# Two matmuls for three in the 256-token feed-forwards: one weight part against both parts of x, halves of a PSUM bank added on the way out

## The chip, the cores and the metric

The kernel runs on one core of one Trainium2 chip. The metric is device time of one execution in microseconds. The engines in what follows: PE (TensorE: matmuls, from SBUF into PSUM), DVE (VectorE), ACT (ScalarE), SP (whose queue issues the loads of weights). PSUM has eight banks of 512 float32 columns on 128 partitions.

## The reference

Two transformer blocks in a row on 256 tokens of 1024 channels, in float32. The first has two layers (a gated short convolution, then neighbourhood attention), each with a feed-forward; the second has four feed-forwards around two mixers:

```python
def swiglu(x, w_in, w_out):
    gate, up = jnp.split(x @ w_in, 2, axis=-1)
    return (jax.nn.silu(gate) * up) @ w_out

for i in range(DEPTH):                                   # second block
    x = x + 0.5 * swiglu(rms_norm(x, ffn1_norm_g[i]), ffn1_w_in[i], ffn1_w_out[i])
    ...                                                  # mixer A (i = 0) or B (i = 1)
    x = x + 0.5 * swiglu(rms_norm(x, ffn2_norm_g[i]), ffn2_w_in[i], ffn2_w_out[i])
```

The hidden width is 2816, so `w_in` is 1024 x 5632 and `w_out` 2816 x 1024.

## The kernel before

**Precision by parts.** PE works on float32r operands. Every weight and every activation is split into a high part, rounded to float32r, and the exact rest, a low part. A product is three matmuls (`mm3`): high x high, high weight x low x, low weight x high x, all summed in the same columns of PSUM. The weights are the stationary operand, the activations the moving one. Activations lie as [128 channels, 8 blocks, 256 tokens], high and low parts in two tiles (`xh`, `xl`; for the hidden values `sh`, `sl`).

**Weights.** `WeightStream` loads them in units of 1024 columns (4 blocks of 128 rows x 256 output columns; 0.5 MB) into five raw buffers. `_split` rounds a unit on ACT (`whi`) and takes the rest on DVE (`wlo`), in two pieces of 512 columns. There are four buffers each for high and low parts. `take()` hands out a unit and first records the splits of the two units behind it.

**A feed-forward of 256 tokens** (`ffn` with n = 256; once in layer 1 of the first block, four times in the second). The hidden part runs over 11 groups of 256 columns; a group takes two units for the gate and two for `up`, each 2 x 4 products. Gate and up of a block of 128 columns lie in the two halves of one bank. Then DVE multiplies a bank with the row of reciprocal norms `R` (second block only), ACT takes silu, DVE the product, and ACT and DVE split the result into `sh`, `sl`. The output part runs over 4 pairs of blocks with 22 products each (six units, the last half as long). `evac` adds a block to the residual `X` on DVE, and behind the second block of a pair `gained` makes the next stage's operand parts (`xh` on ACT, `xl` on DVE) and adds squares into `acc`. So the operands of the next stage are made pair by pair, and its first product needs blocks 0 to 3, its second unit blocks 4 to 7. In the second block the next feed-forward starts at once, and `R` is made behind its first group by `rstd_rows` from `acc` (two products with a constant `mean`, then a Newton iteration on DVE).

**Order.** The code records instructions; a scheduler of the framework puts each engine's in one fixed order. An engine runs them strictly in that order, and a wait on semaphores holds up all behind it. PSUM is parted into a pool of main banks `pm` and one of auxiliary banks `pa`: five and three in feed-forwards, four and four in the mixers; a change closes both pools and opens new ones. The feed-forward of layer 0 runs on 512 tokens (x and context together), with 512-column matmuls.

Of the kernel before, what the change touches and what calls it, by code (L numbers as in the profile page):

```python
# [11 lines left out]
ALU = mybir.AluOpType  # L12
# [54 lines left out]
class WeightStream:  # L67
    """Weights in 0.5 MB units: DRAM -> float32 -> exact float32r parts hi + lo."""
# [24 lines left out]
    def _split(self):  # L93
# [4 lines left out]
        if self.specs[self.split][3]:  # L98
            self.ready.append((v(raw), None, nk, ncol))
        else:  # L100
            hi = self.split_pool.tile([P, self.UNIT], F32R, name="whi", tag="hi")
            lo = self.split_pool.tile([P, self.UNIT], F32R, name="wlo", tag="lo")
            for c0 in range(0, n, 512):
                cs = slice(c0, min(n, c0 + 512))
                self.nc.scalar.copy(hi[:, cs], raw[:, cs])  # L105
                self.nc.vector.tensor_tensor(lo[:, cs], raw[:, cs], hi[:, cs].bitcast(F32), ALU.subtract)  # L106
            self.ready.append((v(hi), v(lo), nk, ncol))
# [13 lines left out]
def cols_units(w, c0, ncol, kblocks, raw=False):  # L121
    """Units that cover the listed blocks of rows for ncol columns, 1024 // ncol blocks each."""
# [21 lines left out]
def mix_units(w, parts):  # L144
    """A product with D columns in sums over parts of the rows."""
# [19 lines left out]
class Net:  # L165
# [27 lines left out]
    def banks(self, nmain, naux):  # L193
# [3 lines left out]
        self.pa = self.psum.enter_context(pool(name="pa", bufs=naux, space=PSUM, reuse_waits="tile"))  # L197

# [19 lines left out]

    def mm3(self, ps, ah, al, bh, bl, first, last):
# [5 lines left out]
    def split(self, hi, lo, src, scale=None):  # L225
        """hi + lo = src (times a per-partition scale), both float32r."""
# [8 lines left out]
    def newton(self, y, a, tag):  # L235
        """y = a ** -0.5."""
# [12 lines left out]
    def wstat(self, pss, xh, xl, kblocks):  # L249
        """pss[c] = W[:, c].T @ x over all listed blocks of rows, weights stationary."""  # L250
# [15 lines left out]
    def xstat_steps(self, bank, tiles, xh, xl, units):  # L266
        """x[:, tile].T @ W for two units of 256 columns, two tiles of tokens in a bank; activations stationary."""
# [7 lines left out]

    def take2(self):
        return [self.ws.take(), self.ws.take()]
# [5 lines left out]
    def partial(self, kblocks, yh, yl, evac):  # L283
        """Sums over kblocks of a product with D columns; evac(j, bank) gets blocks 2j and 2j + 1."""
        j = 0
        while j < KB // 2:
# [4 lines left out]
            banks = [self.main_bank() for _ in range(ncol // T)]  # L291
# [15 lines left out]
    def squares(self, src, acc):  # L307
        """acc + src ** 2 for src of one or two blocks [P, n]."""
# [12 lines left out]
    def rstd_cols(self, accs, ntile, tag):  # L321
        """[P, ntile]: rstd of token tile * 128 + p, from squares [P, tokens] that sum up."""
# [12 lines left out]
    def rows_from_cols(self, r, ntile):  # L335
        """PSUM [P, ntile * 128] with r as a row on every partition."""
# [8 lines left out]
    def rstd_rows(self, acc):  # L345
        """SBUF [P, 2, T]: rstd as a row on every partition, twice; acc [P, 2 * T] of squares."""
        nc = self.nc
        ps = self.aux_bank()
# [4 lines left out]
        R = self.rp.tile([P, 2, T], F32, name="R", tag="R", bufs=1)  # L353
        self.newton(R[:, 0, :], m, "rr")
        nc.vector.tensor_copy(R[:, 1, :], R[:, 0, :])
        return R

    def gained(self, j, gain, xh, xl, acc):
        """Blocks 2j and 2j + 1 of X: operand parts of gain * X, squares into acc."""
        for kb in (2 * j, 2 * j + 1):  # L360
            self.split(xh[:, kb, :], xl[:, kb, :], self.X[:, kb, :], gain[:, kb : kb + 1])
        return self.squares(self.X[:, 2 * j : 2 * j + 2, :], acc)

# [13 lines left out]
    def ada_fast(self, layer, j):  # L377
        """Columns [512 j, 512 j + 512) of the modulation of x and ctx, all on TensorE; yields before its last part."""
# [26 lines left out]
    def ada_columns(self, layer, j, row):  # L405
        """Rows [2, 512] of modulation columns into mod."""
# [7 lines left out]
    def ada_direct(self, layer, j):  # L414
        """The same in float32 products of the weights as they are."""
# [16 lines left out]
    def ada_slow(self, layer, j, vecs):  # L432
        """The same on VectorE, TensorE only sums over partitions; vecs: 1 for x alone, 2 for ctx as well."""
# [43 lines left out]
    def mod_scale(self, layer, which, half):  # L477
        """norm gain * (1 + scale) for half of the blocks."""
# [9 lines left out]
    def row_stats(self, accs, keep=None):  # L488
        """rstd of T tokens as a row on every partition: PSUM [P, T], or copied into keep."""
# [7 lines left out]
    def modulate(self, layer, which, v, src, R, blocks, xh, xl):  # L497
        """Operand parts of modulate(rms(src)) for the listed blocks, in [P, KB, T] views."""
# [17 lines left out]
    def block_squares(self, src, kb, accs):  # L516
        """accs: squares [P, T] that sum up to those of blocks 0..kb."""
# [12 lines left out]
    def ffn(self, xh, xl, sh, sl, n, parts, rows, evac, between=None):  # L530
        """evac(part, j, c, ps) gets block 2j + c of the output; n tokens; rows(): rstd rows or None."""
        nc = self.nc
        R = None
        first = True
        k8 = list(range(8))
        for part, (b0, b1) in enumerate(parts):
            for g in range(b0 // 2, b1 // 2):
                if n == 512:
                    gate = [self.main_bank() for _ in range(2)]
                    up = [self.main_bank() for _ in range(2)]  # L540
                else:
                    both = [self.main_bank() for _ in range(2)]
                    gate = [b[:, :T] for b in both]
                    up = [b[:, T:] for b in both]
                if n == 512 and first:
# [10 lines left out]
                if rows is not None and R is None:  # L556
                    R = rows()
                for c in range(2):
                    blk = 2 * g + c - b0
                    sg = self.tmp()[:, :n]  # L560
                    if R is None:
# [1291 lines left out]
```

## Time and profile before

| | |
|---|---|
| median of 3 runs | 2073.29 us (2072.49 to 2076.35) |
| span of the profiled execution | 2074.1 us |
| PE, DVE, ACT busy | 2039.3, 1481.3, 1048.2 us |
| matmuls | 15070 |
| granted clock of PE, mean | 0.996 |
| feed-forward of layer 1, hidden and output | 855 to 982, 982 to 1045 us |
| first feed-forward of block 2 | 1045 to 1235 us |
| mixer A | 1235 to 1380 us |
| second and third feed-forward | 1380 to 1570, 1570 to 1760 us |
| mixer B | 1760 to 1881 us |
| last feed-forward | 1881 to 2071 us |

The profile gives the profiled execution's span, from its first to its last instruction; that execution's own time on the device is not shown apart from it, and the three times are of other executions. The span is 0.8 us above their median. Of a group of instructions the page shows line, engine, operation, output <- inputs and shapes, the count, then the busy time in us and the mean duration in ns, then the idle time of the engine before them and what ended it. In a timeline the first number is the start in us, the second the length; x2 marks two instructions in a row, merged.

### The profile page before, as it was taken

How to read it: one execution, taken by the hardware profiler on the slowest of the kernel's cores; microseconds unless marked ns; L12 is line 12 of the kernel's file. 1: busy time of each engine (PE TensorE's matmuls, PEld its weight loads, DVE VectorE, ACT ScalarE, POOL GpSimd, SP SyncE). 2: the span in 40 equal slices, each digit the busy share in tenths (PEclk: the TensorE clock that was granted, in tenths of full speed). 3: DMA queues.
4: the chain of work that ended last, by engine and by line, in shares of the span. 5: the costliest groups of instructions: out<-in, count | busy, mean ns of one | idle time of the engine just before them, and what ended most of it. 6: DMA issues, size and time to landing. Idle time of an engine off the chain costs nothing. (4 is left out here: it accounts for less than half of the span.)

```text
span 2074.1 us, 38366 instructions
## 1 busy us (share of the span) xinstructions
PE 2039.3 (98%) x15070; PEld 1912.2 (92%) x15070; DVE 1481.3 (71%) x3177; ACT 1048.2 (51%) x2136; POOL 4.1 (0%) x24
## 2 busy tenths in 40 slices
PE   7999999999999999999999999999999999999999
PEld 3888888888899999999999999999999999989999
DVE  5979998666378778755576657777657665887664
ACT  4534533323355557655455446545545545675443
POOL 0000000000000000000000000000000000000000
PEclk9999999999999999999999999999999999999999
DMA  7746566665254333455565564555556555425554
GB/s 242 231 146 194 182 204 193 222 197 190 83 182 134 91 105 127 156 184 178 181 190 184 177 182 123 158 169 190 180 178 191 185 174 183 143 82 171 185 175 132
DMA packets 327461, 351.33 MB, mean 169 GB/s; under 512 B 12592, under 2 KB 301488, under 8 KB 327280
## 3 DMA queue, kind: packets, MB, share of 16 engines
q1 hardware_dynamic: 327280, 348.88, 53.3%
q8 instruction: 118, 1.93, 0.4%
q14 instruction: 63, 0.52, 0.1%
HBM read 347.78 MB, written 1.05 MB: 168 GB/s over the span
## 5 line engine op out<-in xcount | busy, mean ns | idle before, releaser
L106 DVE TENSOR_TENSOR wlo<-wraw,whi 128x512 fp32r<-128x512 f32 x1121 | 736.5, 685 | 378.6 <-ACT whi L105 374.2
L105 ACT CAST whi<-wraw 128x512 fp32r<-128x512 f32 x1121 | 646.6, 617 | 696.1 <-issue 353.8
L221 PE MATMUL pm<-xh,whi 128*128 128x256 f32 (+1 forms) x2472 | 753.2, 306 | 3.8 <-ACT xh L229 3.2
L222 PE MATMUL pm<-xl,whi 128*128 128x256 f32 (+1 forms) x2472 | 753.4, 305 | 0.2 <-DVE xl L230 0.2
L223 PE MATMUL pm<-xh,wlo 128*128 128x256 f32 (+1 forms) x2472 | 752.9, 305 | 0.0
L221 PEld LDWEIGHTS pm<-xh,whi 128*128 128x128 f32 x2472 | 467.3, 189 | 27.3 <-ACT xh L229 4.4
L222 PEld LDWEIGHTS pm<-xl,whi 128*128 128x128 f32 x2472 | 467.4, 189 | 21.5 <-DVE xl L230 0.6
L223 PEld LDWEIGHTS pm<-xh,wlo 128*128 128x128 f32 x2472 | 467.3, 189 | 21.0
L221 PE MATMUL pm<-sh,whi 128*128 128x256 f32 (+1 forms) x1264 | 368.3, 291 | 0.0
L223 PE MATMUL pm<-sh,wlo 128*128 128x256 f32 (+1 forms) x1264 | 368.2, 291 | 0.0
L222 PE MATMUL pm<-sl,whi 128*128 128x256 f32 (+1 forms) x1264 | 367.9, 291 | 0.0
L221 PEld LDWEIGHTS pm<-sh,whi 128*128 128x128 f32 x1264 | 242.1, 192 | 4.9 <-issue 0.5
L223 PEld LDWEIGHTS pm<-sh,wlo 128*128 128x128 f32 x1264 | 242.1, 192 | 4.2 <-DVE wlo L106 0.2
L222 PEld LDWEIGHTS pm<-sl,whi 128*128 128x128 f32 x1264 | 242.1, 192 | 4.0
L446 DVE SCALAR_TENSOR_TENSOR ada_acc<-wraw,sil,ada_acc 128x512 f32<-128x512 f32 x224 | 159.1, 746 | 21.1 <-DMA wraw<-in_w_ada 19.8
L221 PE MATMUL pm<-whi,xh 128*128 128x256 f32 x576 | 164.9, 286 | 0.0
L223 PE MATMUL pm<-whi,xl 128*128 128x256 f32 x576 | 163.4, 284 | 0.0
L222 PE MATMUL pm<-wlo,xh 128*128 128x256 f32 x576 | 163.0, 283 | 0.1
L221 PEld LDWEIGHTS pm<-whi,xh 128*128 128x128 f32 x576 | 109.6, 190 | 2.6 <-issue 2.5
L222 PEld LDWEIGHTS pm<-wlo,xh 128*128 128x128 f32 x576 | 109.5, 190 | 0.3 <-DVE wlo L106 0.3
L223 PEld LDWEIGHTS pm<-whi,xl 128*128 128x128 f32 x576 | 109.5, 190 | 0.0
L229 ACT CAST sh<-t 128x256 fp32r<-128x256 f32 (+1 forms) x140 | 63.0, 450 | 79.9 <-DVE t L570 68.9
(391 smaller groups left out, 1998.3 us busy)
## 6 DMA issues: line engine op xcount, KB each, us to landing
wraw<-in_ffn_w_in SPq DMA_DIRECT2D x264, 512.0 KB, 4.4
wraw<-in_ffn_w_out SPq DMA_DIRECT2D x128, 512.0 KB, 3.5
wraw<-in_w_ada SPq DMA_DIRECT2D x96, 512.0 KB, 4.4
wraw<-in_a_w_in SPq DMA_DIRECT2D x28, 512.0 KB, 3.6
wraw<-in_conv_w_in SPq DMA_DIRECT2D x24, 512.0 KB, 4.7
wraw<-in_attn_w_qkv SPq DMA_DIRECT2D x24, 512.0 KB, 4.2
wraw<-in_conv_w_out SPq DMA_DIRECT2D x16, 512.0 KB, 4.0
wraw<-in_ffn_w_out SPq DMA_DIRECT2D x28, 256.0 KB, 2.7
```

Of the source, the lines that this page charges most:

```text
L105: self.nc.scalar.copy(hi[:, cs], raw[:, cs])
L106: self.nc.vector.tensor_tensor(lo[:, cs], raw[:, cs], hi[:, cs].bitcast(F32), ALU.subtract)
L221: mm(ps, ah, bh, start=first, stop=False)
L222: mm(ps, ah, bl, start=False, stop=False)
L223: mm(ps, al, bh, start=False, stop=last)
L229: nc.scalar.copy(hi, src)
L446: nc.vector.scalar_tensor_tensor(accs[v], w[:, kk, :], c, accs[v], ALU.mult, ALU.add)
```

## The change

High and low parts of an operand lie side by side: one tile `x2` [128, 8, 2, 256], and `s2` likewise. `pair_unit` multiplies a high weight block with both parts in one 512-column matmul, which fills a bank (half 0: high x high, half 1: high x low), and adds low weight x high part into half 0 with a 256-column matmul. ACT copies the halves 1 of a group's four banks out (`low`), DVE adds them to the halves 0 (`h`) and multiplies by `R`, then silu, product and split go over two blocks at a time. In the output both halves are added to `X`, one after the other. PSUM is two halves of four banks (`half_banks`), used in turn by groups. `rstd_rows` runs after two units of the first group instead of four. `_split` takes a whole unit of 1024 columns in one instruction on ACT and one on DVE, in all stages. The mixers' last output part (`mixer_out`) and `memory_values` use auxiliary banks, and the pools are not opened anew before `mixer_out`.

```diff
 class WeightStream:  # _split
-            for c0 in range(0, n, 512):
-                cs = slice(c0, min(n, c0 + 512))
-                self.nc.scalar.copy(hi[:, cs], raw[:, cs])
-                self.nc.vector.tensor_tensor(lo[:, cs], raw[:, cs], hi[:, cs].bitcast(F32), ALU.subtract)
+            self.nc.scalar.copy(hi[:, :n], raw[:, :n])
+            self.nc.vector.tensor_tensor(lo[:, :n], raw[:, :n], hi[:, :n].bitcast(F32), ALU.subtract)
...
+    def half_banks(self, first):
+        self.psum.close()
+        self.pg = [self.psum.enter_context(self.tc.tile_pool(name=f"pg{i}", bufs=1, space=PSUM, reuse_waits="tile")) for i in range(2)]
+        self.turn = first
+    def group_banks(self):
+        i = self.turn
+        self.turn = 1 - i
+        return self.pg[i].tile([P, 4, 2, T], F32, name=f"pg{i}", tag=f"pg{i}")
...
+    def pair_unit(self, unit, pss, x2, done, nblocks):
+        hi, lo, nk, ncol = unit
+        for c in range(ncol // P):
+            cs = slice(c * P, (c + 1) * P)
+            for kk in range(nk):
+                kb = done + kk
+                self.nc.tensor.matmul(pss[c], hi[:, kk, cs], x2[:, kb], start=kb == 0, stop=False)
+                self.nc.tensor.matmul(pss[c][:, 0, :], lo[:, kk, cs], x2[:, kb, 0, :], start=False, stop=kb == nblocks - 1)
...
+    def ffn_pairs(self, hp, x2, rows, evac, first):
...
+        def hidden(g, ps):
+            low = wide("low", 1)
+            nc.scalar.copy(low, ps[:, :, 1, :])
+            h = wide("h", 2)
+            nc.vector.tensor_tensor(h, ps[:, :, 0, :], low, ALU.add)
+            if rows is not None:
+                nc.vector.tensor_tensor(h, h, env["R"][:, None, :].to_broadcast([P, 4, T]), ALU.mult)
+            yield
+            sg = two(self.tmp())
+            nc.scalar.activation(sg, h[:, 0:2, :], AF.Silu)
+            s = two(self.tmp())
+            nc.vector.tensor_tensor(s, h[:, 2:4, :], sg, ALU.mult)
+            yield
+            self.split(s2[:, 2 * g : 2 * g + 2, 0, :], s2[:, 2 * g : 2 * g + 2, 1, :], s)
+            yield
...
+        for g in range(HB // 2):
+            after = None
+            for u in range(4):
+                unit = self.ws.take()
+                self.pair_unit(unit, [ps[:, u // 2 * 2 + c] for c in range(2)], x2, u % 2 * 4, KB)
+                next(behind, None)
+                if g == 0 and u == 1:
+                    after = self.group_banks()
+                    if rows is not None:
+                        env["R"] = rows(after[:, 0].rearrange("p a t -> p (a t)"))
+            behind = hidden(g, ps)
+            next(behind)
+            ps = after if after is not None else self.group_banks()
...
 def ffn2  # evac
-            nc.vector.scalar_tensor_tensor(x, ps, 0.5, x, ALU.mult, ALU.add)
+            for i in range(2):
+                nc.vector.scalar_tensor_tensor(x, ps[:, i, :], 0.5, x, ALU.mult, ALU.add)
...
 def mixer_out
-    for _ in net.partial(ks, yh, yl, add):
+    for _ in net.partial(ks, yh, yl, add, net.aux_bank):
...
-        net.banks(5, 3)
         return mixer_out(net, MIX_A[-1], yh, yl, gain)
```

How the order moves at the entry from the second to the third feed-forward of block 2 (1570 us before), engine by engine. PE first, in the first group of the third feed-forward; `acc` and `mean` make the statistics. Before:

```order
L221 MATMUL pm<-xh,whi 128x256
L222 MATMUL pm<-xl,whi 128x256
L223 MATMUL pm<-xh,wlo 128x256
L349 MATMUL pa<-acc,mean 128x256
L350 MATMUL pa<-acc,mean 128x256
L221 MATMUL pm<-xh,whi 128x256
L222 MATMUL pm<-xl,whi 128x256
```

Now (the names x_13956 and pg_... are `x2` and a half of PSUM):

```order
L295 MATMUL pg_15646<-x_13956,whi 128x512
L296 MATMUL pg_15646<-x_13956,wlo 128x256
L295 MATMUL pg_15646<-x_13956,whi 128x512
L296 MATMUL pg_15646<-x_13956,wlo 128x256
L370 MATMUL pg_15691<-acc,mean 128x256
L371 MATMUL pg_15691<-acc,mean 128x256
L295 MATMUL pg_15646<-x_13956,whi 128x512
L296 MATMUL pg_15646<-x_13956,wlo 128x256
```

Two matmuls stand for three, and the statistics stand after two units of the group instead of four.

ACT at the same place: `whi` rows are splits of weights, `xh` (now x_13956) the operand of the third feed-forward, the row behind it the squares. Before:

```order
L232 ACTIVATE xh<-X,pk 128x256 x2
L313 ACTIVATE t<-X 128x512
L105 CAST whi<-wraw 128x512 x11
L232 ACTIVATE xh<-X,pk 128x256 x2
L313 ACTIVATE t<-X 128x512
```

Now:

```order
L242 ACTIVATE x_13956<-X,pk 128x256 x2
L335 ACTIVATE t<-X 128x512
L103 CAST whi<-wraw 128x1024
L103 CAST whi<-wraw 128x512
L103 CAST whi<-wraw 128x1024 x5
L242 ACTIVATE x_13956<-X,pk 128x256 x2
L335 ACTIVATE t<-X 128x512
```

Eleven half units were the last two units of the output part (one of them short) and four of the next stage; now five of the next stage stand ahead of the casts of blocks 6 and 7.

DVE at the same place; `X` rows are the additions to the residual, L352 (now L373) reads the statistics. Before:

```order
L106 TENSOR_TENSOR wlo<-wraw,whi 128x512 x9
L1137 SCALAR_TENSOR_TENSOR X<-pm,X 128x256 x2
L106 TENSOR_TENSOR wlo<-wraw,whi 128x512
L233 SCALAR_TENSOR_TENSOR xl<-X,pk,xh 128x256 x2
L106 TENSOR_TENSOR wlo<-wraw,whi 128x512
L318 TENSOR_TENSOR acc<-acc,t 128x512
L106 TENSOR_TENSOR wlo<-wraw,whi 128x512 x8
L352 TENSOR_SCALAR t<-pa 128x256
```

Now:

```order
L104 TENSOR_TENSOR wlo<-wraw,whi 128x1024 x3
L1193 SCALAR_TENSOR_TENSOR X<-pg_15359,X 128x256
L104 TENSOR_TENSOR wlo<-wraw,whi 128x1024
L1193 SCALAR_TENSOR_TENSOR X<-pg_15359,X 128x256 x3
L104 TENSOR_TENSOR wlo<-wraw,whi 128x1024
L243 SCALAR_TENSOR_TENSOR x_13956<-X,pk,x_13956 128x256 x2
L340 TENSOR_TENSOR acc<-acc,t 128x512
L373 TENSOR_SCALAR t<-pg_15691 128x256
```

The fourth unit of the next stage stands between the four additions, and the fifth ahead of the two low parts.

More of the change, by code (lines that the diff above doesn't have):

```diff
@@ L290, in partial @@
                 units.append(self.ws.take())
-            banks = [self.main_bank() for _ in range(ncol // T)]
+            banks = [(bank or self.main_bank)() for _ in range(ncol // T)]
             for c in range(ncol // P):
@@ L527, in block_squares, with ffn @@
         return [new]
-    def ffn(self, xh, xl, sh, sl, n, parts, rows, evac, between=None):
+    def ffn(self, xh, xl, sh, sl, parts, evac, between):
         nc = self.nc
-        R = None
         first = True
@@ L537, in ffn @@
             for g in range(b0 // 2, b1 // 2):
[L538 to L545, printed above, removed]
+                gate = [self.main_bank() for _ in range(2)]
+                up = [self.main_bank() for _ in range(2)]
+                if first:
                     units = [self.ws.take() for _ in range(4)]
@@ L1254, in mixer_out @@
 def mixer_out(net, ks, yh, yl, gain):
-    nxh, nxl = net.next_x()
+    nx2 = net.next_x()
     st = {"acc": None}
```

132 lines of the change are left out of this document (68 added, 64 removed).

## The prediction

> **What bounds the kernel now.** First the page's span and engine shares, then the waits of TensorE (PE), then a table by stretch, then the order in time at the places where one stage hands over to the next.
>
> ```profile
> span 2074.1 us, 38366 instructions
> PE 2039.3 (98%) x15070; PEld 1912.2 (92%) x15070; DVE 1481.3 (71%) x3177; ACT 1048.2 (51%) x2136; POOL 4.1 (0%) x24
> PEclk9999999999999999999999999999999999999999
> PE pm L221 <- ACT xh L229: 3.2, 3, 1.9
> PE pm L221 <- DVE X L1246: 0.9, 1, 0.9
> ```
>
> PE is busy for 98% of the span at a granted clock that never falls below nine tenths, and the largest waits of its product line L221 are single microseconds. So the time is the sum of what each matmul takes, and a busy share does not say what that is: matmuls overlap. The distance from one start to the next does. In a table by stretch, x counts the matmuls that touch the stretch, so the distance is (length + duration of one) / count; the durations stand in the groups by line.
>
> ```profile
> L221 PE MATMUL pm<-xh,whi 128*128 128x256 f32 x1952 | 551.2, 283 | 3.0 <-ACT xh L229 2.3 <-ACT whi L105 0.6
> L221 PE MATMUL pm<-xh,whi 128*128 128x512 f32 x512 | 199.2, 392 | 0.8 <-ACT xh L229 0.8
> core 0: us, PE busy (x), PEclk, DMA share, GB/s
> 451.00:471.00 20.00, 20.00 (x90) 1.00 0.64 203
> 862.00:980.00 118.00, 118.00 (x986) 1.00 0.61 192
> 985.00:1043.00 58.00, 58.00 (x486) 1.00 0.59 186
> 1395.00:1505.00 110.00, 110.00 (x929) 1.00 0.58 181
> 1510.00:1569.00 59.00, 59.00 (x494) 1.00 0.58 183
> ```
>
> The first stretch is the 512-token feed-forward: (20 + 0.39) / 90 = 226.6 ns for 512 columns. The others are feed-forwards of 256 tokens: 118.28 / 986 = 120.0 and 58.28 / 486 = 119.9 ns in the one of attention (hidden, output), 110.28 / 929 = 118.7 and 59.28 / 494 = 120.0 ns in one of block 2. Doubling the columns adds 106.6 ns, so about 13.4 ns of each matmul does not depend on its columns.
>
> **The change, part by part.** *A. Three matmuls become two.* A feed-forward has 11 x 4 x 8 = 352 products in the hidden part and 8 x 22 = 176 in the output, 2640 in all five. Each was three 256-column matmuls and becomes one of 512 and one of 256: 226.6 + 120.0 = 346.6 ns. Before: 3 x 120.0 = 360.0, and 3 x 118.7 = 356.1 in the hidden parts of block 2. Attention's feed-forward gains 528 x 13.4 = 7.1 us; each of the four others 352 x 9.5 + 176 x 13.4 = 5.7 us. Sum 29.9 us, all of it on the path, since PE has no slack there. No row has the two widths in turn. Bounds: with 118.7 for the narrow one the sum is 29.9 + 2640 x 0.0013 = 33.3 us; if columns alone counted (the same 768 are streamed) it is 0. I take the first, since both widths have a steady pace of their own.
>
> The Trainium skill speaks against this term: "TensorE: Matmul & The Clock Gate", section "Back-to-back issue gap", gives N / 2.4 + 2.5 ns at full clock, by which a matmul saved is worth 2.5 ns and all 2640 some 6.6 us. The rows above, 120.0 and 226.6 against its 109.2 and 215.8, do not agree with it here; its constant is the isolated gap without a weight load, and the measurement decides.
>
> *B. The vector and scalar work of a group.* It is hidden if a group of four units still fits in PE's 32 x 0.3466 = 11.1 us.
>
> ```profile
> L106 DVE TENSOR_TENSOR wlo<-wraw,whi 128x512 fp32r<-128x512 f32 x132 | 86.8, 686 | 58.5 <-ACT whi L105 57.7
> L570 DVE TENSOR_TENSOR t<-t 128x256 f32<-128x256 f32 x22 | 9.3, 421 | 4.9 <-ACT t L567 4.9
> L105 ACT CAST whi<-wraw 128x512 fp32r<-128x512 f32 x132 | 75.7, 617 | 72.3 <-issue 40.5 <-PE pm L222 29.6 <-ACT whi L105 1.4
> L229 ACT CAST sh<-t 128x256 fp32r<-128x256 f32 x22 | 8.9, 404 | 6.9 <-DVE t L570 6.9
> 1573.30 1.89 DVE L106 TENSOR_TENSOR wlo<-wraw,whi 128x512 fp32r<-128x512 f32 x3
> 1578.77 1.14 ACT L105 CAST whi<-wraw 128x512 fp32r<-128x512 f32 x2 [1.66 <-PE pm L222]
> ```
>
> VectorE (DVE) takes 686 ns for 512 columns and 421 for 256; back to back it issues one every (1.89 - 0.69) / 2 = 0.60 us. So I estimate a 1024-column instruction at 686 + 2 x 265 = 1216 ns, one every 1.13; its bounds are the same 1.13 and two halves, 1.20. ScalarE (ACT) by the same working: 617 + 2 x 213 = 1043 ns, one every 0.95 (two halves: 1.14 - 0.62 + 0.52 = 1.04). A group costs DVE four splits, the addition of the halves and the product with `R` at 1.13 and two of 512 at 0.60, 8.0 us; ACT four splits and `low` at 0.95 and two of 512, 5.8 us. Both fit into 11.1, and PSUM's other half is needed only a group later. In the output a block pair costs DVE 5 x 1.13 + 0.60 for weights, four additions, two low parts and the squares, under 10 us of PE's 44 x 0.3466 = 15.3. I cost B at nothing inside the stages; if that cover fails, PE waits group by group (rival 4).
>
> *C. The hand-over from one feed-forward to the next.* Here PE has always had the next operand in time:
>
> ```profile
> 1570.02 0.28 PE L223 MATMUL pm<-sh,wlo 128*128 128x256 f32 x1
> 1570.14 0.28 PE L221 MATMUL pm<-xh,whi 128*128 128x256 f32 x1
> 1570.22 0.62 ACT L105 CAST whi<-wraw 128x512 fp32r<-128x512 f32 x1 [0.30 <-PE pm L222]
> 1570.75 0.90 ACT L232 ACTIVATE xh<-X,pk 128x256 fp32r<-128x256 f32 x2
> 1570.04 0.75 DVE L1137 SCALAR_TENSOR_TENSOR X<-pm,X 128x256 f32<-128x256 f32 x2
> 1571.31 0.88 DVE L233 SCALAR_TENSOR_TENSOR xl<-X,pk,xh 128x256 fp32r<-128x256 f32 x2
> 1572.70 0.68 DVE L318 TENSOR_TENSOR acc<-acc,t 128x512 f32<-128x512 f32 x1
> 1581.53 0.59 PE L349 MATMUL pa<-acc,mean 128*128 128x256 f32 x2
> ```
>
> The low parts of blocks 6 and 7 end at 1572.19. PE reaches block 6 after its first unit and blocks 4 and 5 of the second, 30 matmuls or 3.5 us after 1570.14, at 1573.7: 1.5 us of slack. In the new order (shown with the change) ACT splits one more unit, the fifth of the next stage, ahead of the two operand casts. That unit's buffer is the first unit's, free when PE has done its last wide matmul: 7 x 0.347 + 0.39 = 2.8 us after the start. Counting from PE's start in the stage from 1570: the cast of weights ends at 2.86 + 1.04 = 3.9; DVE's split of that unit, which also stands ahead, takes 3.95 to 5.1; the low part of block 6 ends at 5.1 + 0.48 = 5.6. PE needs it at 10 x 0.347 = 3.5: a wait of 2.1 us. At the entry from attention's feed-forward the DVE split stands behind the low parts, so only ACT's place counts: operand cast 3.8 to 4.3, low part 4.8, wait 1.4 us. At the entry to mixer A the fourth unit's split stands between the four additions: cast 0.3 to 1.35, split to 2.6, three additions (0.335 apart) to 3.6, low parts at 4.1 and 4.8 against 3.7 and 4.5, 0.8 us. At the entry to mixer B no split stands between, and the mixers hand over to feed-forwards with one addition as before: nothing. Sum 4.3 us; bounds 0 (if the scheduler's spacing holds ACT's work earlier than I think) and, with every one of the seven entries paying 2.1, 14.7.
>
> The statistics rows (L349) move from after four units to after two. `acc` would come 1.3 us behind block 7's low part, at about 6.6, and PE, itself held to 5.6, reaches them at 7.6: nothing. They are the same matmuls as before and stay.
>
> *D. Gaps that the old PSUM pools made.*
>
> ```profile
> 1234.41 0.28 PE L223 MATMUL pm<-sh,wlo 128*128 128x256 f32 x1
> 1235.32 0.36 PE L221 MATMUL pm<-xh,whi 128*128 128x256 f32 x1 [0.64 <-ACT whi L105]
> 1367.88 0.28 PE L223 MATMUL pm<-yh,wlo 128*128 128x256 f32 x1
> 1369.04 0.35 PE L221 MATMUL pm<-yh,whi 128*128 128x256 f32 x1 [0.88 <-DVE X L1246]
> ```
>
> Before mixer A and before its last output part PE stood for 0.91 and 1.16 us between starts, beyond the 0.12 of a matmul 0.8 and 1.0. At both places banks changed hands; afterwards the mixer starts in the half that has long been empty, and the output part uses banks that are open already. I take 0.7 and 0.9 back (ends 0 and 1.8), 1.6 us.
>
> *E. The ends.* In the last feed-forward the final block takes two additions instead of one:
>
> ```profile
> 2070.58 0.28 PE L223 MATMUL pm<-sh,wlo 128*128 128x256 f32 x1
> 2070.89 0.42 DVE L1137 SCALAR_TENSOR_TENSOR X<-pm,X 128x256 f32<-128x256 f32 x1 [0.29 <-PE pm L223]
> ```
>
> so 0.4 us more. At the start, where the first units are awaited, a unit is whole after 1.04 + 1.22 = 2.26 us on ACT and DVE, against 0.62 + 0.52 + 0.69 = 1.83 in two halves: 0.4 us more once (ends 0 and 1). In the mixers the split of a whole unit frees 0.07 us of DVE and 0.1 of ACT, and can hold up a short chain by 0.53 more; I take these as equal.
>
> **Sum.** 2074.1 - 29.9 + 4.3 - 1.6 + 0.8 = 2047.7 us for this execution. Its span lies 0.8 above the median of the three times, 2073.29, so 2047 us.
>
> **Rivals.**
> 1. *No new waits, narrow matmuls at 118.7.* Terms C and E vanish and A is 33.3: 2074.1 - 33.3 - 1.6 = 2039. The unchanged slack of 1.5 us speaks for it, the order of ACT against it.
> 2. *Entries and mixers cost more.* Attention's mixing and both mixers take some 107 units. If one in five of their splits holds the chain up by its extra 0.53 us, that is 11 us; the entries at twice the price add 4: 2047.7 + 15 = 2063, less still than before. For it: DVE is busy there for four fifths of the time and PE waits on short chains. Against it: DVE and ACT have less to do in all.
> 3. *Columns alone count.* The pair takes as long as the triple, A is 0 and the waits stay: 2074.1 + 4.3 - 1.6 + 0.8 = 2077.6, within 0.2% of before. It needs the 13.4 ns to belong to the 256 columns, against the 512-column row. The Trainium skill's gap, quoted above ("TensorE: Matmul & The Clock Gate", "Back-to-back issue gap"), comes near this case: by it the time would be 2071.
> 4. *The other side: DVE becomes the bound in the hidden groups.* If a 1024-column instruction took p instead of 1.13, a group would cost DVE 6 p + 1.2. Above p = 1.65 that is over PE's 11.1, and above p = 1.73 (55 groups, each losing 0.48) the whole gain of 26.4 is gone. At p = 2.0 it is 13.2, 2.1 lost in each of 55 groups: 2047.7 + 116 = 2163. Its place would be the addition that reads four banks of PSUM and the product with a repeated `R`. Against it: the row of 128x512 `t<-pm,R`, which reads PSUM, is no slower than the split of weights:
>
> ```profile
> L566 DVE TENSOR_TENSOR t<-pm,R 128x512 f32<-128x512 f32 x22 | 15.0, 683 | 0.0
> ```
>
> **Chances.** The forecast 0.70, rival 1 0.10, rival 2 0.12, rival 3 0.03, rival 4 0.05. Rivals 3 and 4 together are under one in ten, so the range reaches over most of 1 and half of 2: 2038 to 2059. About 0.2%, 4 us, is what a measurement of this kernel can tell from no change. Faster 0.70 + 0.10 + 0.12 = 0.92, the same 0.03, slower 0.05.
>
> **What would show it.** A: matmuls start 346 to 347 ns apart per pair in the hidden and output stretches; 360 would be rival 3. B: PE has no wait on `low`, `h` or weights inside a stage; waits that return every 11 to 12 us would be rival 4, and the mean of the 1024-column DVE groups tells its price at once (1216 ns, or near 2000). C: waits of PE on the low part of the operand, once at each of three entries, 1 to 2 us. D: the two gaps at mixer A are gone. The prediction fails if the pair is not the sum of its two widths, or if the mixers' stretches change by more than some microseconds.

## The result: 3.1% slower, and the profile after

The changed kernel takes 2139.38 us (median of four runs, 2133.12 to 2142.92) against 2072.89 for the kernel before in the same runs: a ratio of 1.0311, interval 1.0291 to 1.0331. The forecast was 2047 us, faster.

Three lines of the page after, to be held against the first ones of the prediction:

```profile
span 2137.1 us, 31972 instructions
PE 2051.0 (96%) x12430; PEld 1799.1 (84%) x12430; DVE 1517.3 (71%) x2568; ACT 1043.2 (49%) x1535; POOL 4.1 (0%) x24
PEclk9999999999999999999999999999999999999999
```

PE has 2640 matmuls fewer and is busy 12 us longer, in a span 63 us longer. The clock in tenths of the span still reads 9 everywhere: a loss of some microseconds at a time doesn't show there. (Nor did it in the kernel before: its clock was 0.50 from 1250.3 to 1253.7 us, so the prediction's "never falls below nine tenths" holds for the fortieths of the span only.) The waits of PE show the loss (what PE waits for, then total, times, longest, in us):

```profile
PE pg L295 <- DVE X L1193: 28.6, 8, 3.6
PE pa L349 <- DVE acc L340: 11.4, 1, 11.4
PE pg L295 <- DVE X L534: 7.7, 2, 3.8
PE pa L349 <- DVE acc L546: 5.5, 2, 4.0
PE pa L364 <- DVE t L362: 3.7, 3, 2.7
PE pg L295 <- DVE x L243: 3.2, 2, 2.0
```

The last line is the wait that the prediction named (term C). The second is no news: the kernel before has it too, with 11.7 us. The first and the third were not in the prediction: ten stops of 3.55 to 3.84 us, two in each of the five feed-forwards, where a wide matmul waits for DVE's additions to `X`. One of them in the order of time, PE first, then DVE:

```profile
1208.46 0.28 PE L296 MATMUL pg<-s,wlo 128*128 128x256 f32 x1
1212.34 0.76 PE L295 MATMUL pg<-s,whi 128*128 128x512 f32 x1 [3.60 <-DVE X L1193]
```

```profile
1208.38 1.23 DVE L104 TENSOR_TENSOR wlo<-wraw,whi 128x1024 fp32r<-128x1024 f32 x1 [1.60 <-ACT whi L103]
1209.52 0.42 DVE L1193 SCALAR_TENSOR_TENSOR X<-pg,X 128x256 f32<-128x256 f32 x1
1209.85 1.22 DVE L104 TENSOR_TENSOR wlo<-wraw,whi 128x1024 fp32r<-128x1024 f32 x1
1210.98 1.21 DVE L1193 SCALAR_TENSOR_TENSOR X<-pg,X 128x256 f32<-128x256 f32 x3
```

The matmul at 1212.34 is the first of the output's second pair of blocks. It writes banks 2 and 3 of a half; the additions read banks 0 and 1. It starts only when the fourth addition is done, because the four banks are one tile (`pg`). The additions take 1.6 us, the two weight splits among them 2.4. By stretch, in the same place (busy time and count of PE, of its weight loads, of DVE, ACT and POOL, then the granted clock):

```profile
1205.00:1208.40 3.40, 3.40 (x21) 2.99 (x20) 1.25 (x2) 1.56 (x2) 0.00 (x0) 1.00 0.33 99
1208.40:1212.20 3.80, 0.34 (x2) 0.02 (x1) 3.77 (x7) 1.55 (x2) 0.00 (x0) 0.90 0.71 231
1212.20:1215.00 2.80, 2.66 (x8) 2.31 (x9) 1.30 (x3) 1.03 (x2) 0.00 (x0) 0.50 0.75 215
1215.00:1218.00 3.00, 3.00 (x11) 2.53 (x10) 0.00 (x0) 0.34 (x1) 0.00 (x0) 0.50 0.02 6
1218.00:1221.00 3.00, 3.00 (x18) 2.62 (x17) 1.23 (x1) 0.86 (x2) 0.00 (x0) 0.95 0.00 0
```

Behind this stop the clock is 0.50 for some 6 us, and 3 us hold 11 matmuls instead of 18. So this stop costs more than its wait. The Trainium skill has this on its page "TensorE: Matmul & The Clock Gate", section "HAM oscillation — how this bites in real kernels": idle gaps of more than about 3.4 us send the array back to half clock. These rows agree with it. The trace as a whole agrees only in part: behind two of the ten stops the clock stayed at 1.00, and behind one wait of 1.98 us it fell (rows in the last section).

The stages from one first matmul to the next, in us, of the kernel before, the changed one and two of the experiments below:

| stage | before | after | three mends | with banks in turn |
|---|---|---|---|---|
| up to attention's feed-forward | 853.5 | 869.1 | 853.3 | 853.9 |
| attention's feed-forward | 191.5 | 197.8 | 190.1 | 185.3 |
| first of block 2 | 190.3 | 201.1 | 188.1 | 184.5 |
| mixer A | 145.3 | 147.2 | 144.3 | 142.9 |
| second, third of block 2 | 189.5, 189.5 | 195.5, 201.5 | 186.6, 188.2 | 184.8, 185.2 |
| mixer B | 121.5 | 124.3 | 124.2 | 123.4 |
| last feed-forward | 189.4 | 195.7 | 186.5 | 184.7 |
| behind the last matmul's start | 3.5 | 4.9 | 4.8 | 4.9 |

### The profile page after: what moved, and what is told of

The parts are those of the page before. It is cut to its first block, busy times and chain, and to the rows that moved or that the text cites. A ratio compares the mean times of both kernels' runs of the same rounds, so it can differ in the third digit from the quotient of the medians.

```text
span 2137.1 us, 31972 instructions
## 1 busy us (share of the span) xinstructions
PE 2051.0 (96%) x12430; PEld 1799.1 (84%) x12430; DVE 1517.3 (71%) x2568; ACT 1043.2 (49%) x1535; POOL 4.1 (0%) x24
## 4 chain that ended last, share of the span: by engine, by line
PE 84%; DVE 8%; ACT 4%; issue 2%; DMA 2%; SPq 0%; DVEq 0%; ACTq 0%
PE pg L295 29%; PE pg L296 15%; PE pm L232 11%; PE pm L231 11%; PE pm L233 11%; DVE wlo L104 3%; PE pa L231 2%; PE pa L232 1%; PE pa L233 1%; ACT whi L103 1%; DVE ada_acc L466 1%; DMA wraw<-in_w_ada 1%; DVE X L1193 1%; ACT t L528 1%; PE pa L443 0%
## 5 line engine op out<-in xcount | busy, mean ns | idle before, releaser
L104 DVE TENSOR_TENSOR wlo<-wraw,whi 128x1024 fp32r<-128x1024 f32 (+1 forms) x575 | 686.4, 1195 | 416.5 <-ACT whi L103 414.3
L103 ACT CAST whi<-wraw 128x1024 fp32r<-128x1024 f32 (+1 forms) x575 | 589.8, 1027 | 767.9 <-PE pg L295 279.0
L295 PE MATMUL pg<-x,whi 128*128 128x512 f32 x1408 | 496.6, 395 | 3.2 <-DVE x L243 3.2
L296 PE MATMUL pg<-x,wlo 128*128 128x256 f32 x1408 | 398.7, 283 | 0.0
L295 PE MATMUL pg<-s,whi 128*128 128x512 f32 x880 | 326.1, 412 | 36.3 <-DVE X L1193 28.6
L295 PEld LDWEIGHTS pg<-x,whi 128*128 128x128 f32 x1408 | 264.8, 188 | 65.2 <-DVE x L243 4.1
L296 PEld LDWEIGHTS pg<-x,wlo 128*128 128x128 f32 x1408 | 265.1, 188 | 0.1
L231 PE MATMUL pm<-xh,whi 128*128 128x512 f32 (+1 forms) x576 | 216.1, 380 | 1.2 <-ACT xh L239 1.2
L231 PEld LDWEIGHTS pm<-xh,whi 128*128 128x128 f32 x576 | 108.7, 190 | 23.9 <-ACT xh L239 2.3
L233 PEld LDWEIGHTS pm<-xh,wlo 128*128 128x128 f32 x576 | 108.6, 189 | 21.7 <-DVE wlo L104 1.3
L232 PEld LDWEIGHTS pm<-xl,whi 128*128 128x128 f32 x576 | 108.7, 189 | 20.7 <-DVE xl L240 0.5
L231 PE MATMUL pm<-sh,whi 128*128 128x256 f32 (+1 forms) x384 | 119.2, 311 | 0.2 <-ACT whi L103 0.2
```

What stands on the lines that cost most here:

```text
L103: self.nc.scalar.copy(hi[:, :n], raw[:, :n])
L104: self.nc.vector.tensor_tensor(lo[:, :n], raw[:, :n], hi[:, :n].bitcast(F32), ALU.subtract)
L231: mm(ps, ah, bh, start=first, stop=False)
L232: mm(ps, ah, bl, start=False, stop=False)
L233: mm(ps, al, bh, start=False, stop=last)
L295: self.nc.tensor.matmul(pss[c], hi[:, kk, cs], x2[:, kb], start=kb == 0, stop=False)
```

## The experiments

The theories: (1) the output's pairs wait for each other through a tile; (2) `memory_values` in auxiliary banks stands behind the norm statistics; (3) splits of a whole unit hold up short chains; (4) wide and narrow matmuls in turn don't keep the pace that each has by itself. Each stands against the rival that its expectation names.

**New halves in the output.** The changed kernel, with

```diff
-            if j == 2:
+            if j > 0:
                 ps = self.group_banks()
-            pss = [ps[:, j % 2 * 2 + c] for c in range(2)]
+            pss = [ps[:, c] for c in range(2)]
```

> One edit to the changed kernel: every output pair takes a new half of PSUM, so no pair shares a tile with the pair before it. Theory 1 (a half is one tile, and the second pair of a half waits for all additions that read the first, although they read other banks): the ten stops of about 3.75 us go, and with them the slow matmuls behind each. The five output parts, 364 us together, come to 5 x 176 x 0.353 = 311, so 2139 - 53 = 2086 us, between 2080 and 2092. Rival (the additions themselves are late, or DVE is full there, so the wait only moves to another instruction): less than 10 us, above 2129.

2082.8 us, 1.0042 of before (1.0029 to 1.0056): 56.6 us off the changed kernel. The first two lines of the waits above are gone. DVE does the same in the same order in the same place:

```profile
1196.86 0.42 DVE L1193 SCALAR_TENSOR_TENSOR X<-pg,X 128x256 f32<-128x256 f32 x1
1197.19 1.21 DVE L104 TENSOR_TENSOR wlo<-wraw,whi 128x1024 fp32r<-128x1024 f32 x1
1198.32 1.20 DVE L1193 SCALAR_TENSOR_TENSOR X<-pg,X 128x256 f32<-128x256 f32 x3
```

and PE goes from the last matmul of one pair of blocks to the first of the next without a stop:

```profile
1195.80 0.28 PE L296 MATMUL pg<-s,wlo 128*128 128x256 f32 x1
1195.92 0.40 PE L295 MATMUL pg<-s,whi 128*128 128x512 f32 x1
```
The additions were never late for anything but the shared tile: theory 1 is shown. The five output parts fall from 363.8 to 310.8 us, 53.0, of which the waits were 36.3. The clock behind them explains most of the rest: in these parts of the changed kernel it was 0.50 for 41 us, some 37 of them with matmuls running, and at 12 matmuls instead of 19 in 3.4 us (rows in the last section) that is 14 us, an estimate.

**Main banks for memory_values.** The changed kernel, with

```diff
 def memory_values
-        bank = net.aux_bank()
+        bank = net.main_bank()
```

> One edit to the changed kernel: memory_values takes main banks again, as before the change; by the order its first product then stands on TensorE ahead of the norm statistics instead of behind them. Theory 2 (the changed banks cost the entry to attention's feed-forward 7 us of idle and some slow matmuls behind it): attention's feed-forward starts 7 to 10 us earlier, near 861 instead of 869, and the time is 2139 - 9 = 2130 us, between 2127 and 2133. Rival (the 14 us by which that feed-forward starts late come from the attention stage ahead of it, and the products only move): within 2 us of 2139.

2139.3 us, no difference to the changed kernel: a miss. The products did move ahead of the statistics, but attention's feed-forward begins at 869.7, since a new wait stands before it:

```profile
PE pg L295 <- DVE mvl L243: 8.8, 1, 8.8
```

`mvl` is made from the banks of these products; they lie in the half of PSUM that the feed-forward opens first. The rival isn't shown by that either, so the theory was tried once more with other banks, further down.

**Whole-unit splits in the kernel before.** The kernel before, with

```diff
-            for c0 in range(0, n, 512):
-                cs = slice(c0, min(n, c0 + 512))
-                self.nc.scalar.copy(hi[:, cs], raw[:, cs])
-                self.nc.vector.tensor_tensor(lo[:, cs], raw[:, cs], hi[:, cs].bitcast(F32), ALU.subtract)
+            self.nc.scalar.copy(hi[:, :n], raw[:, :n])
+            self.nc.vector.tensor_tensor(lo[:, :n], raw[:, :n], hi[:, :n].bitcast(F32), ALU.subtract)
```

> The kernel before with one edit: a weight unit is split in one instruction of 1024 columns on ACT and one on DVE instead of two each. Theory 3 (whole-unit splits hold up short chains in attention's mixing and the two mixers): 5 us later at attention's feed-forward, 2 and 3 us in mixers A and B and about 2 at entries between feed-forwards, so 2073 + 10 = 2083 us, between 2078 and 2088. Rival (the splits cost nothing, and those 10 us come from the other parts of the change or from the order that the scheduler chose): within 4 us of 2073.

2084.7 us, 1.0047 (1.0032 to 1.0062): 10.1 us slower by this alone. Attention's feed-forward begins at 859.2 instead of 853.5, mixer A takes 1.9 more, mixer B 1.4; the feed-forwards are the same to 0.1 us. (In mixer B the clock was 0.50 for 3.4 us, which it wasn't there in the kernel before, so how much of the 1.4 is the splits' is not shown.) Theory 3 is shown, and its place is the mixing, not the hand-over between feed-forwards.

**Runs of one width.** New halves in the output, and in `pair_unit`

```diff
             for kk in range(nk):
                 kb = done + kk
                 self.nc.tensor.matmul(pss[c], hi[:, kk, cs], x2[:, kb], start=kb == 0, stop=False)
+            for kk in range(nk):
+                kb = done + kk
                 self.nc.tensor.matmul(pss[c][:, 0, :], lo[:, kk, cs], x2[:, kb, 0, :], start=False, stop=kb == nblocks - 1)
```

> The kernel with new halves in the output, and a second edit: within a unit and a column block the four 512-column matmuls stand first and the four 256-column ones behind them, instead of in turn. Theory 4 (taking the widths in turn costs some 6 ns a pair: in the changed kernel 233 + 120 = 353 where each width by itself would give 226.6 + 120.0 = 346.6): pairs at 347 to 349 ns, 2640 x 0.005 = 13 us less than the kernel with new halves alone, so 13 us below it. Rival (the rest of 6 ns belongs to the wide matmul whatever stands beside it, or to DVE and PSUM traffic): the same pace of 353 and the same time within 3 us.

2079.8 us, 1.0029 (1.0018 to 1.0040), 3.0 below the kernel with new halves, where 13 were expected. Four wide ones in a row still start 232 to 233 ns apart and four narrow ones 118 to 119: neither side is met. Either a wide matmul is slower in the new layout, or four in a row are too few.

**Splits of 512 columns again.** New halves in the output, and the diff of the whole-unit splits the other way round.

> The kernel with new halves in the output, with weights split in two instructions of 512 columns again. Theory 3 as the run on the kernel before left it (whole-unit splits cost 5.7 us ahead of attention's feed-forward, 1.9 in mixer A, 1.4 in mixer B): 2082.8 - 9 = 2074 us, between 2070 and 2077; attention's feed-forward starts near 862 instead of 867.5. It also holds that the entry waits between feed-forwards (1.4 and 2.1 us of PE on the low part of the operand) come from the whole unit that ACT casts first: they fall below 0.5 us. Rival (in the new PSUM order the short chains are held up by something else): within 4 us of 2082.8.

2070.4 us, 0.9985 (0.9976 to 0.9993): 12.4 us off, at the lower edge of what was expected. Attention's feed-forward begins at 860.1. The entries improve only in part: the waits on the low part of the operand are 0.3 and 0.6 at one of them (one stop of 1.4 before) and 1.1 at the other (2.0 before), not below 0.5. ACT still casts a unit of weights between the two operand casts there; half the size, it costs half the wait.

**Own banks for memory_values.** New halves in the output, whole-unit splits, and

```diff
-        net.banks(5, 3)
+        net.banks(4, 2)
+        net.pv = net.psum.enter_context(tc.tile_pool(name="pv", bufs=2, space=PSUM, reuse_waits="tile"))
 def memory_values
-        bank = net.aux_bank()
+        bank = net.pv.tile([P, 512], F32, name="pv", tag="pv")
```

> The kernel with new halves in the output, and two banks of the upper half kept for memory_values alone (pools of 4, 2 and 2), whole-unit splits as in the changed kernel. Theory 2 in its second form (memory_values on main banks gains 7 us and loses 8.8 again, because the first half of PSUM that the feed-forward opens then waits for DVE to read those banks; in banks of the upper half of its own it would keep the gain): the products stand ahead of the norm statistics, no wait on mvl, attention's feed-forward starts near 860 instead of 867.5 and the time is 2082.8 - 8 = 2075 us, between 2072 and 2078. Rival (the chain to the feed-forward's operand ends at the same time whatever PE does meanwhile): the products merely fill the idle time, less than 3 us.

2077.0 us, 1.0014 (1.0005 to 1.0023): 5.8 us below the kernel with new halves, and attention's feed-forward begins at 860.9 instead of 867.5. In the changed kernel PE stood idle there while DVE made the statistics, with the products of `memory_values` (L231, `pa`) queued behind, and the clock was 0.50 from 849.7 to 859.9:

```profile
845.83 0.28 PE L233 MATMUL pm<-oh,wlo 128*128 128x256 f32 x1
850.14 0.59 PE L349 MATMUL pa<-mean,acc 128*128 128x1 f32 x2 [4.04 <-DVE acc L546]
...
854.75 1.22 PE L364 MATMUL pa<-t,ones 128*128 128x256 f32 x2 [2.73 <-DVE t L362]
855.41 0.78 PE L231 MATMUL pa<-whi,xl 128*128 128x256 f32 x1
```

In the banks of their own (`pv`) they stand ahead and fill that time, as in the kernel before, and the statistics no longer wait:

```profile
846.26 0.28 PE L231 MATMUL pv<-whi,xl 128*128 128x256 f32 x1
...
850.59 0.28 PE L349 MATMUL pa<-mean,acc 128*128 128x1 f32 x2
```

Theory 2 holds in this second form.

**The three mends together** (new halves, own banks, splits of 512).

> New halves in the output, own banks for memory_values, and weights split by 512 columns: the three mends together. If all three theories hold and add up: 2139.4 - 56.6 - 9 - 8 = 2066 us, 0.4% below the kernel before, between 2062 and 2070. If the mends overlap in attention (the same idle time counted twice): 2071 to 2074, no difference to the kernel before that can be measured.

2064.1 us, 0.9950 (0.9937 to 0.9963), faster than before. The gains add up. This is the change without its three side effects, and so the measure of what it is worth itself: some 10 us, 8 to 13 by the interval of the ratio.

**Patterns.** New halves in the output, and in each feed-forward another order of matmuls, read by time per product.

```diff
 def pair_unit  # wide(c, kk): high weight times x2; slim(c, kk): low weight times the high part
+        if self.stage == 0:    # per product: wide, then low weight times both parts, 512 columns as well
+        if self.stage == 1:    # three 256-column matmuls (the first product of a block: wide, slim)
+        if self.stage == 2:    # per unit: all wide ones, then all slim ones
+        if self.stage == 3:    # wide, slim, slim, wide
+        if self.stage == 4:    # per row block: wide on both banks, slim on both banks
```

> The kernel with new halves in the output; each of the five feed-forwards issues its matmuls in another pattern, to be read as time per product. First, all 512 columns wide (low weight times both parts of x, one part more than needed); second, three 256-column matmuls in the new layout, as before the change; third, eight wide ones, then eight narrow ones per unit; fourth, wide narrow, narrow wide, so that like stands beside like; fifth, wide on one bank, wide on the other, then both narrow. Theory 4 mended (each width keeps 226.6 and 120.0 only in a row of its like, and each change of width costs 2 to 4 ns): 453, 360 or 356, 348, 350, 350 ns. Rival (a wide matmul costs 233 in the new layout whatever stands beside it): 466, 356 to 360, 351 to 353, 353, 353 ns.

One stretch of each, the first feed-forward with two (hidden, output), the others of their output parts:

```profile
880.00:1020.00 140.00, 140.00 (x619) 115.97 (x618) 71.85 (x69) 60.72 (x69) 0.00 (x0) 1.00 0.47 144
1030.00:1100.00 70.00, 70.00 (x310) 57.97 (x310) 34.48 (x45) 25.69 (x32) 0.00 (x0) 1.00 0.48 147
1240.00:1290.00 50.00, 50.00 (x421) 49.72 (x420) 29.84 (x42) 23.36 (x30) 0.00 (x0) 1.00 0.62 185
1570.00:1620.00 50.00, 50.00 (x288) 43.90 (x288) 31.46 (x44) 23.93 (x31) 0.00 (x0) 1.00 0.60 189
1760.00:1810.00 50.00, 50.00 (x289) 43.65 (x288) 30.32 (x42) 22.86 (x29) 0.00 (x0) 1.00 0.63 194
2070.00:2115.00 45.00, 45.00 (x260) 39.23 (x259) 24.46 (x30) 16.85 (x18) 0.00 (x0) 1.00 0.53 163
```

As in the prediction, (length + one matmul) / count is the distance; one is 0.39 us, 0.28 or, of a pair, 0.34 on the mean. All wide: 140.39 / 619 and 70.39 / 310, 227 ns a matmul, 454 a product: the new layout costs a wide matmul nothing, and the rival is out. Runs of a unit 349.6, mirrored 348.4, by banks 348.8, against 351 to 354 for wide and narrow in turn (rows two runs below). That is theory 4 in direction, but the cost doesn't follow the number of changes of width: runs of eight change least and are not the quickest; in the hidden part of the same feed-forward they gained nothing (90.34 / 514 x 2 = 351.5 ns, from 1460 to 1550 us). The triple here took 50.28 / 421 x 2.955 matmuls a product = 353, less than the 360 in the kernel before, so the pair seemed to gain nothing at all; hence the run after next.

**The three mends, and banks in turn.**

```diff
 def pair_unit
+        cols = [slice(c * P, (c + 1) * P) for c in range(ncol // P)]
+        for kk in range(nk):
+            kb = done + kk
+            for c, cs in enumerate(cols):
+                self.nc.tensor.matmul(pss[c], hi[:, kk, cs], x2[:, kb], start=kb == 0, stop=False)
+            for c, cs in enumerate(cols):
+                self.nc.tensor.matmul(pss[c][:, 0, :], lo[:, kk, cs], x2[:, kb, 0, :], start=False, stop=kb == nblocks - 1)
```

> The kernel with the three mends, and a fourth: in a unit the matmuls go wide on one bank, wide on the other, narrow on the one, narrow on the other. The look at the patterns gave 347.6 ns a product for this order against 353.4 for wide and narrow in turn. If that holds in all five feed-forwards: 2640 x 0.0055 = 14 us less, 2064 - 14 = 2050 us, between 2046 and 2055. Rival (the pace of single stages shifts, but waits behind the matmuls take it back): within 4 us of 2064.

2050.4 us, 0.9883 (0.9869 to 0.9896): the best of all, 1.2% below the kernel before, and 13.7 us of it by an order of instructions alone. In the hidden and output parts of two feed-forwards:

```profile
890.00:970.00 80.00, 80.00 (x462) 69.79 (x461) 55.61 (x80) 47.63 (x80) 0.00 (x0) 1.00 0.63 189
980.00:1035.00 55.00, 55.00 (x318) 47.98 (x317) 35.69 (x63) 27.37 (x49) 0.00 (x0) 1.00 0.60 187
1390.00:1480.00 90.00, 90.00 (x518) 78.81 (x517) 68.89 (x97) 53.91 (x90) 0.00 (x0) 1.00 0.62 189
1495.00:1545.00 50.00, 50.00 (x289) 43.60 (x289) 31.77 (x59) 25.42 (x47) 0.00 (x0) 1.00 0.63 196
```

348 to 349 ns a product in all four, near the 346.6 of term A.

**The three mends, but triples.** `pair_unit` in turn as in the change, past a block's first product with

```diff
-                self.nc.tensor.matmul(pss[c], hi[:, kk, cs], x2[:, kb], start=kb == 0, stop=False)
+                    for i in range(2):
+                        self.nc.tensor.matmul(pss[c][:, i, :], hi[:, kk, cs], x2[:, kb, i, :], start=False, stop=False)
```

> The kernel with the three mends, but every product past the first of a block as three 256-column matmuls again, into the same halves of a bank; the work on the way out stays. It asks what two matmuls for three are worth by themselves. If nothing (the pattern run had 353.4 ns for three narrow ones in an output part, as much as the pair): 2064 us, between 2061 and 2069. If the triple takes 360 in this layout too, as in the kernel before: 2640 x 0.0066 = 17 us more, 2081.

2074.2 us, 0.9997 (0.9988 to 1.0006), between the two: triples cost 0.47% more than pairs in turn, 9.7 us by the two ratios (each with about 3 us of interval). The stretches of the triples, and below them those of the pairs (the kernel with the three mends):

```profile
890.00:970.00 80.00, 80.00 (x645) 78.75 (x644) 53.04 (x78) 45.45 (x78) 0.00 (x0) 1.00 0.61 185
985.00:1040.00 55.00, 55.00 (x455) 54.73 (x455) 32.98 (x61) 26.18 (x48) 0.00 (x0) 1.00 0.61 188
1390.00:1480.00 90.00, 90.00 (x733) 88.57 (x732) 68.41 (x97) 53.81 (x89) 0.00 (x0) 1.00 0.62 188
1505.00:1560.00 55.00, 55.00 (x455) 54.72 (x455) 34.16 (x62) 26.34 (x49) 0.00 (x0) 1.00 0.60 187
```

```profile
890.00:970.00 80.00, 80.00 (x455) 69.38 (x454) 53.86 (x77) 46.36 (x78) 0.00 (x0) 1.00 0.62 186
985.00:1040.00 55.00, 55.00 (x313) 47.72 (x312) 34.24 (x62) 27.20 (x50) 0.00 (x0) 1.00 0.61 188
1390.00:1480.00 90.00, 90.00 (x514) 78.94 (x514) 68.93 (x97) 54.26 (x89) 0.00 (x0) 1.00 0.63 190
1505.00:1555.00 50.00, 50.00 (x285) 43.41 (x284) 32.12 (x59) 25.07 (x45) 0.00 (x0) 1.00 0.61 194
```

With 2.875 matmuls a product in the hidden parts and 2.955 in the output ones (a block's first product is a pair), the triple takes 357.8, 359.0, 354.1 and 359.0 ns; the pair 353.1, 353.6, 351.5 and 353.3. Over the parts that is 352 x 4.7 + 4 x 352 x 2.6 + 880 x 5.5 ns = 10.2 us. The 353 of the pattern run was one stage's peculiarity: the same stage has it here too (62.2 us for 176 products), no other has (63.2). Why is open.

**Banks in turn in the kernel before.** In `wstat_unit` the same loops, three kinds of products by two banks.

> The kernel before with one edit: the three matmuls of a product alternate between the two banks of a unit (high weights times high x on both banks, then the next kind on both). If the order and not the widths makes part of the pace, the 256-column triples fall from 360 and 356 towards 350 ns: 2640 x 0.007 = 18 us less, 2056. If a narrow matmul takes 118.7 to 120.0 in a row of its like, in whatever bank: 2074, within 4 us.

2084.8 us, 1.0046 (1.0032 to 1.0061). In a hidden part of attention's feed-forward and one of block 2:

```profile
890.00:980.00 90.00, 90.00 (x753) 90.00 (x752) 50.45 (x93) 45.66 (x94) 0.00 (x0) 1.00 0.60 182
1395.00:1505.00 110.00, 110.00 (x926) 109.89 (x925) 77.72 (x145) 57.84 (x115) 0.00 (x0) 1.00 0.60 187
```

90.28 / 753 = 119.9 and 110.28 / 926 = 119.1 ns: narrow matmuls keep their pace whatever bank they go to, as the second theory had it. So what banks in turn mend is the mixture of widths. The time lies some 11 us above even the second expectation. The edit also reorders the convolution and the mixers' projections, and the loss lies outside the feed-forwards: that of attention begins 6.7 us later, both mixers take longer. Why was not followed further.

## Why the prediction was wrong

The forecast lies 92.4 us below the measured time. Four steps account for most of it.

1. *Term B, "PSUM's other half is needed only a group later ... I cost B at nothing inside the stages": 56.6 us.* In the hidden groups the sentence held: DVE's and ACT's prices came out as estimated (1223 and 1050 ns against 1216 and 1043), and nothing waited ahead of `h`:

```profile
L104 DVE TENSOR_TENSOR wlo<-wraw,whi 128x1024 fp32r<-128x1024 f32 x546 | 666.8, 1223 | 391.9 <-ACT whi L103 389.7
L103 ACT CAST whi<-wraw 128x1024 fp32r<-128x1024 f32 x546 | 572.3, 1050 | 727.5 <-PE pg L295 259.1 <-PE pm L232 185.2 <-issue 174.0
L612 DVE TENSOR_TENSOR h<-pg,low 128x1024 f32<-128x1024 f32 x55 | 67.0, 1217 | 0.0
```

   In the output it failed. There two pairs use one half one after the other, as the code says (`if j == 2`), and the cover was added up as work per pair (under 10 us of 15.3) without asking when the last reader lets go of the tile. Rival 4 had PE waiting for DVE, but for DVE's throughput in the hidden groups; here DVE stood idle for 1.6 us just ahead of the stop.

2. *Term A, 29.9 us, came to 14.7: 15 us.* The step that failed is "I take the first, since both widths have a steady pace of their own". In turn, wide and narrow take 351.5 to 353.6 ns, not 346.6. Against the triples of the kernel before that is 352 x 6.9 + 1408 x 4.6 + 880 x 6.6 ns = 14.7 us. Two matmuls for three by themselves gave 9.7 to 10.2 of it; the rest is that triples, too, are a little quicker in the new layout (354 to 359 ns for 356 to 360), which is not explained. The bounds (0 to 33.3) held it, the choice inside them was wrong. The Trainium skill's gap ("TensorE: Matmul & The Clock Gate", "Back-to-back issue gap"), set aside in the prediction, gave 6.6 us, an estimate by its 2.5 ns, for two matmuls in place of three: nearer to the measured 9.7, though its constants fit neither pace. In another order the pair does reach 348 to 349.

3. *Term E's last sentence, whole-unit splits in the mixers "I take these as equal": 10 us.* Measured alone in the kernel before: 10.1, of which 5.7 ahead of attention's feed-forward; taken back in the changed order, with shorter waits at the entries, 12.4. Rival 2 had this mechanism at 11 us and a chance of 0.12.

4. *A part of the change that had no term: 6 us.* `memory_values` in auxiliary banks was told and not priced. It moved 96 matmuls from one side of a wait to the other: 5.8 and 6.2 us by the two runs that move them back.

Together 56.6 + 15 + 10 + 6 = 88 us of the 92.4. The other 4 were not measured apart; 1 of them is E's tail, and 2 to 3 lie in mixer B.

What was right: most of C, with waits of 1.2 and 2.0 us in the changed kernel at the two entries where 1.4 and 2.1 were worked out. Mixer A's 0.8 did not come: in its first 13 us no two starts lie more than 0.25 us apart. D: the two gaps at mixer A are gone. E's tail was +1.4 instead of +0.4, because four additions stand behind the last matmul and not two (the last pair of blocks shares a tile, and the additions of its first block come after that matmul as well):

```profile
2132.55 1.67 DVE L1193 SCALAR_TENSOR_TENSOR X<-pg,X 128x256 f32<-128x256 f32 x4 [8.66 <-PE pg L296]
```

Left open: why a mixture of widths is slower than its parts, and 2 to 3 us in mixer B that no mend gave back. In the kernel with the three mends the clock was 0.50 there in two stretches of 3.4 us, in the kernel before in none; by 12 matmuls instead of 19 that would be 2.5 us, an estimate. What lowered it is not shown, and no run took back the mixers' auxiliary banks.

## What to carry to other kernels

Where several banks are one tile, ask of every user which other user of the tile has to end first: work that is hidden by volume can still stop the matmuls if it is the last to read a shared tile. A change that carries side edits (a coarser split, other banks for a neighbour) needs a price for each, since here three side effects cost 75 us (2139.4 against 2064.1) and the idea itself brought 10. And the pace of a new sequence is not the sum of the paces of its parts: measure the sequence, and try its order, which was worth 14 us more.

## What the runs showed of the hardware

Matmuls of 512 and 256 columns keep 227 and 119 to 120 ns in rows of their like; taken in turn a pair costs 351 to 354 ns, with starts that in the output parts of the kernel with new halves repeat in a cycle of three pairs (236 + 113, 233 + 117, 241 + 120), and 348 to 349 when two of a width stand side by side on two banks. Runs of four of a width gave little (3 us), runs of eight 349.6 in an output part and nothing in a hidden part.

Behind a stop of PE the granted clock often falls to 0.50, for 3.4 or 6.8 us, but the length of the wait alone doesn't decide it. Of the ten stops of 3.55 to 3.84 us in the changed kernel eight have such a stretch behind them; those that ended at 1595.44 and 2080.34 have none. A wait of 1.98 us that ended at 1616.41 has one; a wait of 1.96 us that ended at 1579.25, in the kernel with new halves (last row), has none:

```profile
1595.40:1598.80 3.40, 3.36 (x19) 3.00 (x20) 1.47 (x3) 1.35 (x3) 0.00 (x0) 1.00 0.60 182
1617.70:1621.10 3.40, 3.40 (x12) 2.83 (x10) 0.00 (x0) 1.04 (x1) 0.00 (x0) 0.50 0.41 136
```

```profile
1579.30:1581.00 1.70, 1.70 (x9) 1.47 (x10) 0.90 (x2) 0.00 (x0) 0.00 (x0) 1.00 0.74 194
```
